# Token sums of the seven-product up projection: formed during two plain f-tiles, the fourth kept in DRAM, and the down phase's loads in another order

## The chip, the cores and the metric

The kernel runs on one core of a Trainium2 chip. A core has TensorE (PE) for matmuls, VectorE (DVE), ScalarE (ACT), GpSimd (POOL) and SyncE (SP), which issues nearly all DMAs of this kernel. The metric is the device time of one execution in microseconds (us), lower being better; three runs of the kernel before have a median of 2636.69 us.

## The reference: what is computed

One inference step of a streaming encoder with two layers, in fp32, for 1152 tokens (a prompt of 1024 and 8 running streams of 16) of width 1024. Layer 0 mixes tokens by a gated recurrence beside a differential attention, layer 1 by trailing-window means. Behind either mixer stands the same feed-forward block, and the change is in that block alone. The width of its hidden layer, D_FF, is 2816:

```python
def conv_ffn(x, hist, w_up, conv_w, conv_b, w_down):
    T = x.shape[1]
    a, b = jnp.split(x @ w_up, 2, axis=-1)
    ah = jnp.concatenate([hist.astype(x.dtype), a], axis=1)
    c = conv_b
    for j in range(CONV_W):
        c = c + ah[:, j:j + T] * conv_w[j]
    return (jax.nn.silu(c) * b) @ w_down, ah[:, -(CONV_W - 1):]
```

Its result is added to the scaled input, and the sum is normalised over the width.

## The kernel before

**Products of three.** An fp32 operand is kept as two parts, `hi` (the value cast to fp32r) and `lo` (the rest). `split` makes them: ACT casts `hi`, VectorE subtracts to get `lo` (GpSimd does it for most weights, by `split_half`). `mm3` then issues three matmuls: hi by hi, hi by lo, lo by hi. The activations stand transposed in SBUF as `xh` and `xl`, 8 blocks of 128 rows (k = 0 to 7) by 1152 tokens.

**The up phase (`ffn_up`).** The 22 f-tiles of 128 hidden columns come one after another. The first two (`PLAIN = 2`, L1180) are plain: for the two halves a and b of `w_up`, three chunks of 384 tokens and 8 blocks of k, 144 matmuls of 128x384. The other 20 use seven products in place of eight (`SEVEN`, L1183), the tokens being cut into halves h0 and h1 and k into two halves: 168 matmuls of 128x288 per f-tile, in the order x00, t3, t2, x10, t1, t4, x11 of their token operands. The first three token sums t1, t2 and t3 have tiles of their own and are made by `combine(kk)` (L1273) for each of the four slices kk of 128x576, one slice behind each of the first four chunks of the second plain tile. t4 takes the place of x01, that is `xh` and `xl` at [0:4, h1], which plain tiles still read; so `combine_last(kk)` (L1285) makes it behind the last plain tile, during the first four products.

The weights of each seven-product tile are loaded by `fetch` (L1302) to one of three `raw` tiles and summed and split by `prepare` (L1309), five products ahead (`AHEAD`): VectorE forms the sums (L1320 to L1324), ACT `hi`, GpSimd `lo`. The results of a tile are gathered in `ext` (the half a) and `bb` (the half b), in part by ACT's copies and in part by VectorE's additions (L1375 to L1385). `conv(f)` (L1212) makes the convolution, SiLU and the product with `bb` from them, beside the next f-tile, and stores the row f of 128x1152 in DRAM as `g_scr`.

**The down phase (`ffn_down`).** It reads the rows of `g_scr` back (`graw`, one buffer, 576 KB), splits them into `gh` (ACT) and `gl` (VectorE), and adds their products with `w_down` into nine tiles `acc` of 512 KB, which hold the block's input, loaded from `x_scr`. Rows come in groups of two. Its first loads are emitted inside the up phase: `leave()`, two products before its end, frees the tiles of t1 to t3 and runs `ffn_down` to its first `yield`; `open_acc` opens the nine tiles and loads them, each `fetch` loads a row's weights and its `graw`.

```python
1406         acc = open_acc(lambda t: scr_rows(l, t))
...
1442         ready = [fetch(f) for f in GROUPS[0]]
1443         yield acc
```

**What sets the order.** A scheduler places the instructions on the engines by their dependencies and the order in which they are emitted; each engine then works through its own queue in order, and SP's DMAs start in SP's order. A tile with one buffer is rewritten only when its last reader is done.

Of the kernel before, what the change touches and what calls it, by code (L numbers as in the profile page):

```python
# [10 lines left out]
F32 = mybir.dt.float32  # L11
F32R = mybir.dt.float32r
# [98 lines left out]
def hybrid_stream_kernel(ctx: ExitStack, tc: tile.TileContext, i, o, k):  # L111
# [42 lines left out]
    def split(hi, lo, src, sub=None):  # L154
        nc.scalar.copy(hi, src)  # L155
        (sub or nc.vector).tensor_tensor(lo, src, hi, ALU.subtract)  # L156

    def raw_tile(name="raw"):
        return wp.tile([128, 1024], F32, tag="raw", name=name, bufs=3)
# [108 lines left out]
    def drain(g):  # L268
        for _ in g:
            pass  # L270

    def chain(*gens):
        for g in gens:
            yield from g
# [16 lines left out]
    oa_scr = dr.tile([NTOK, 512], F32, name="oa_scr")  # L291
    ob_scr = dr.tile([NTOK, 512], F32, name="ob_scr")
    x_scr = [dr.tile([NTOK, D], F32, name=f"x_scr{l}") for l in range(2)]
    g_scr = [dr.tile([NF, 128, NTOK], F32, name=f"g_scr{l}") for l in range(2)]
    w_in = i["w_in_ab"][0].rearrange("(k p) c -> p k c", p=128)

# [778 lines left out]

    acc_s = []

    def open_acc(rows):

        acc_s.append(ExitStack())  # L1080
        accp = pool_of(acc_s[0], "accp", 1)
        tiles = [accp.tile([128, D], F32, name=f"acc{t}") for t in range(NT)]
        for t in range(NT):
            nc.sync.dma_start(tiles[t], rows(t))
        return tiles

    def close_acc():
        acc_s.pop().close()
# [1 line left out]
    def scr_rows(l, t):  # L1090
        return x_scr[l][t * 128:(t + 1) * 128, :]

    with ExitStack() as ph:
# [42 lines left out]
        last_gate = gate(NPT, so.tile([128, H, 128], F32, tag="gate", name="gt"))  # L1136
        drain(running)
        at_s.close()
        acc = open_acc(x_rows)
        sp = pool_of(ph, "sp", 2, side="right")  # L1140
        sums = sp.tile([128, NT, 4], F32, name="sums", bufs=1)

# [34 lines left out]


    HALF = NTOK // 2
    PLAIN = 2  # L1180


    SEVEN = (("a0", "x00", 0, True), ("s3", "t3", 1, True), ("s2", "t2", 0, False), ("a1", "x10", 2, True),  # L1183
# [3 lines left out]
    def ffn_up(l, acc, late, first, leave):  # L1187
# [44 lines left out]
        def plain(f, w, order):  # L1232

            _, _, bb = begin(f)
            for part, c in order:
                a, n = CHUNKS[c]
                p = bank([128, n], "pu")
                for kk in range(KD):
                    mm3(p, w[part][0][kk], w[part][1][kk], xh[:, kk, a:a + n], xl[:, kk, a:a + n],
                        kk == 0, kk == KD - 1)  # L1240
                if part == 0:
                    put_a(f, a, p, n)
                else:
                    nc.vector.tensor_copy(bb[:, a:a + n], p)
                yield
# [24 lines left out]
        def temp(n):  # L1270
            return tmp.tile([128, HALF], F32, tag=n, name=n)

        def combine(kk):  # L1273

            A, B, C = temp("sa"), temp("sb"), temp("sc")
            nc.vector.tensor_tensor(A, xh[:, kk, h0], xl[:, kk, h0], ALU.add)
            nc.gpsimd.tensor_tensor(B, xh[:, kk, h1], xl[:, kk, h1], ALU.add)
            nc.gpsimd.tensor_tensor(C, xh[:, 4 + kk, h1], xl[:, 4 + kk, h1], ALU.add)
            nc.vector.tensor_tensor(A, B, A, ALU.subtract)
            nc.vector.tensor_tensor(B, C, B, ALU.subtract)  # L1280
            nc.vector.tensor_tensor(C, C, A, ALU.subtract)
            for n, src in (("t3", B), ("t2", C), ("t1", A)):
                split(tt[n][0][:, kk], tt[n][1][:, kk], src)

        def combine_last(kk):  # L1285
            A, B = temp("sa"), temp("sb")
            nc.gpsimd.tensor_tensor(A, xh[:, 4 + kk, h0], xl[:, 4 + kk, h0], ALU.add)
            nc.vector.tensor_tensor(B, tt["t2"][0][:, kk], tt["t2"][1][:, kk], ALU.add)
            nc.vector.tensor_tensor(A, A, B, ALU.subtract)
            split(xh[:, kk, h1], xl[:, kk, h1], A)  # L1290

        def tokens(n, q, c):
            cs = slice(c * (HALF // 2), (c + 1) * (HALF // 2))
# [8 lines left out]
        def fetch(f, part):  # L1302
            raw = raw_tile()
            nc.sync.dma_start(raw.rearrange("p (k c) -> p k c", c=128), up_cols(l, part * FF + f * 128))
            raws[f, part] = raw
# [20 lines left out]
                   "s3": b[:, up], "s4": a[:, lo]}[name]  # L1326
            wts[n] = [x.rearrange("p (k c) -> p k c", c=128) for x in split_half(src)]

        u = plain(1, second, [(p, c) for p in range(2) for c in range(3)])
        side = conv(0)  # L1330
        for s in range(6):
            next(u)
            if s < 4:
                combine(s)
            if s in (0, 2):
                next(side, None)
            if s in (1, 2):
                fetch(PLAIN, s - 1)
            if s >= 4:
                prepare(s - 4)  # L1340
        drain(u)
        drain(side)
        fetch(PLAIN + 1, 0)
        for n in range(2, AHEAD):
            prepare(n)

        banks = {}
        n_last = 7 * (NF - PLAIN) - 1
        side = conv(1)
        H2 = HALF // 2  # L1350
        for n in range(n_last + 1):
            f, m = PLAIN + n // 7, n % 7
            if m == 0:
                begin(f)
            if n < 4:
                combine_last(n)
            prepare(n + AHEAD)
            if m == 0 and f + 1 < NF:
                fetch(f + 1, 1)
            if m == 2 and f + 2 < NF:  # L1360
                fetch(f + 2, 0)
            _, tok, bi, starts = SEVEN[m]
            ext, _, bb = open_f[f]
            wh, wl = wts.pop(n)
            for c in range(2):
                if starts:
                    banks[bi, c] = bank([128, H2], "pu")
                p = banks[bi, c]
                for q in range(4):
                    th, tl = tokens(tok, q, c)  # L1370
                    mm3(p, wh[:, q], wl[:, q], th, tl, starts and q == 0, q == 3)
                a0, a1 = c * H2, HALF + c * H2
                e0, b0, b1 = ext[:, 2 + a0:2 + a0 + H2], bb[:, a0:a0 + H2], bb[:, a1:a1 + H2]
                if m == 0:
                    nc.scalar.copy(e0, p)  # L1375
                elif m == 1:
                    nc.scalar.copy(b1, p)
                elif m == 2:
                    nc.scalar.copy(b0, p)
                elif m == 3:  # L1380
                    nc.vector.tensor_tensor(e0, e0, p, ALU.add)
                elif m == 4:
                    nc.vector.tensor_tensor(b1, b1, p, ALU.add)  # L1383
                elif m == 5:
                    nc.vector.tensor_tensor(b0, b0, p, ALU.add)  # L1385
                else:
                    put_a(f, a1, p, H2)
            if n == n_last - 2:
                tmp_s.close()
                tt_s.close()  # L1390
                leave()
            if m in (0, 1, 2, 3, 4):
                next(side, None)
            if m == 6:
                drain(side)
                side = conv(f)
# [5 lines left out]
    def ffn_down(l, last, ahead):  # L1402


        d_s = ExitStack()
        acc = open_acc(lambda t: scr_rows(l, t))
        cp = pool_of(d_s, f"fc{l}", 2)
        gpools = [pool_of(d_s, f"ga{l}", 2)]

# [30 lines left out]
                yield  # L1440

        ready = [fetch(f) for f in GROUPS[0]]
        yield acc
        gpools.append(pool_of(d_s, f"gb{l}", 2, side="right"))
        cq = pool_of(d_s, f"fd{l}", 1, side="right")
# [220 lines left out]
```

## Time and profile before

| | before |
|---|---|
| median of three runs | 2636.69 us (2636.11 to 2640.91) |
| the profiled execution | 2637.27 us |
| its span | 2635.1 us |
| granted TensorE clock, mean | 0.976 |
| TensorE busy | 2514.0 us, 95% of the span |
| VectorE busy | 1561.9 us, 59% |
| ScalarE, GpSimd busy | 1080.1 us, 960.6 us |

The up phase of layer 0 is read here around 925 to 1050 us of the span, where plain tiles give way to seven-product ones, and around 1414 to 1443 us, where the down phase follows. The same places of layer 1 lie at 1858 us and 2337 us. In a table by stretch, busy time is given for each engine with its count of instructions; the granted clock is a share of full speed, so 1.00 is 2.4 GHz. A matmul's row in a timeline shows when it started and how long it lasted; since matmuls overlap, the time from one start to the next is what one costs. Times in square brackets are what the engine was idle just before, and whom it waited for.

### The profile page before, as it was taken

How to read it: one execution, taken by the hardware profiler on the slowest of the kernel's cores; microseconds unless marked ns; L12 is line 12 of the kernel's file. 1: busy time of each engine (PE TensorE's matmuls, PEld its weight loads, DVE VectorE, ACT ScalarE, POOL GpSimd, SP SyncE). 2: the span in 40 equal slices, each digit the busy share in tenths (PEclk: the TensorE clock that was granted, in tenths of full speed). 3: DMA queues.
4: the chain of work that ended last, by engine and by line, in shares of the span. 5: the costliest groups of instructions: out<-in, count | busy, mean ns of one | idle time of the engine just before them, and what ended most of it. 6: DMA issues, size and time to landing. Idle time of an engine off the chain costs nothing. (4 is left out here: it accounts for less than half of the span.)

```text
span 2635.1 us, 45541 instructions
## 1 busy us (share of the span) xinstructions
PE 2514.0 (95%) x18138; PEld 2309.4 (88%) x18138; DVE 1561.9 (59%) x2728; ACT 1080.1 (41%) x2192; POOL 960.6 (36%) x735
## 2 busy tenths in 40 slices
PE   8999999999999889999998999989799999989997
PEld 8999987886889889999997788879799999977886
DVE  3377753338983685555554665788755555456557
ACT  2255545355762534444443121365344444431113
POOL 1111111006642555554553122244555555521222
PEclk9999999998999989999999999989899999999998
DMA  5744357777674212222224222232122222252222
GB/s 167 200 115 121 87 171 248 221 256 241 230 229 174 104 35 66 76 76 76 76 76 182 89 94 83 69 92 81 51 76 76 76 75 76 75 186 96 93 77 81
DMA packets 275123, 314.36 MB, mean 119 GB/s; under 512 B 46059, under 2 KB 209460, under 8 KB 274911
## 3 DMA queue, kind: packets, MB, share of 16 engines
q1 hardware_dynamic: 272485, 309.82, 36.2%
q8 instruction: 143, 2.34, 0.4%
q10 hardware_dynamic: 2426, 1.63, 0.3%
q14 instruction: 69, 0.57, 0.1%
HBM read 239.66 MB, written 71.74 MB: 118 GB/s over the span
## 5 line engine op out<-in xcount | busy, mean ns | idle before, releaser
L156 POOL TENSOR_TENSOR lo<-raw,hi 128x512 fp32r<-128x512 f32 x364 | 517.1, 1433 | 1128.5 <-ACT hi L155 985.3
L155 ACT CAST hi<-raw 128x512 fp32r<-128x512 f32 x380 | 231.6, 620 | 573.3 <-PE pu L143 275.9
L143 PE MATMUL pu<-xh,hi 128*128 128x288 f32 (+1 forms) x1472 | 444.9, 303 | 9.9 <-DVE bb L1383 9.4
L143 PE MATMUL pu<-xl,hi 128*128 128x288 f32 (+1 forms) x1472 | 444.4, 302 | 3.0 <-DVE xl L156 3.0
L143 PE MATMUL pu<-xh,lo 128*128 128x288 f32 (+1 forms) x1472 | 444.2, 302 | 0.0
L143 PE MATMUL pd<-hi,gh 128*128 128x512 f32 x792 | 315.7, 399 | 21.7 <-ACT gh L155 21.7
L143 PE MATMUL pd<-lo,gh 128*128 128x512 f32 x792 | 317.2, 401 | 0.0
L143 PE MATMUL pd<-hi,gl 128*128 128x512 f32 x792 | 313.3, 396 | 0.0
L1435 DVE TENSOR_TENSOR acc<-acc,pd 128x512 f32<-128x512 f32 x330 | 216.6, 682 | 122.5 <-PE pd L143 122.2
L143 PEld LDWEIGHTS pu<-xh,hi 128*128 128x128 f32 x1472 | 278.8, 190 | 11.3 <-DVE bb L1383 10.4
L143 PEld LDWEIGHTS pu<-xl,hi 128*128 128x128 f32 x1472 | 279.2, 190 | 3.6 <-DVE xl L156 3.6
L143 PEld LDWEIGHTS pu<-xh,lo 128*128 128x128 f32 x1472 | 279.2, 190 | 0.0
L143 PE MATMUL ptm<-hi,xh 128*128 128x256 f32 x720 | 209.5, 291 | 4.2 <-ACT hi L155 4.2
L143 PEld LDWEIGHTS pd<-hi,gh 128*128 128x128 f32 x792 | 150.2, 190 | 60.4 <-ACT gh L155 22.6
L143 PE MATMUL ptm<-lo,xh 128*128 128x256 f32 x720 | 202.1, 281 | 0.1
L143 PE MATMUL ptm<-hi,xl 128*128 128x256 f32 x720 | 201.9, 281 | 0.0
L1222 DVE SCALAR_TENSOR_TENSOR cv<-ext,prm,cv 128x1024 f32<-128x1024 f32 (+1 forms) x176 | 178.0, 1066 | 28.9 <-ACT cv L1219 28.8
L143 PEld LDWEIGHTS pd<-hi,gl 128*128 128x128 f32 x792 | 149.8, 189 | 36.7 <-DVE gl L156 1.2
L143 PEld LDWEIGHTS pd<-lo,gh 128*128 128x128 f32 x792 | 150.1, 190 | 34.3
L143 PEld LDWEIGHTS ptm<-hi,xh 128*128 128x128 f32 x720 | 136.5, 190 | 7.4 <-ACT hi L155 4.6
L143 PEld LDWEIGHTS ptm<-lo,xh 128*128 128x128 f32 x720 | 136.6, 190 | 0.9 <-DVE lo L156 0.4
L143 PEld LDWEIGHTS ptm<-hi,xl 128*128 128x128 f32 x720 | 136.2, 189 | 0.0
(332 smaller groups left out, 5886.3 us busy)
## 6 DMA issues: line engine op xcount, KB each, us to landing
raw<-in_ffn_w_up SPq DMA_DIRECT2D x88, 512.0 KB
kraw<-in_cache_k SPq DMA_DIRECT2D x64, 512.0 KB
vraw<-in_cache_v SPq DMA_DIRECT2D x64, 512.0 KB
g_scr<-cv SPq DMA_DIRECT2D x44, 576.0 KB
graw<-g_scr SPq DMA_DIRECT2D x44, 576.0 KB
raw<-in_ffn_w_down SPq DMA_DIRECT2D x44, 512.0 KB
raw<-in_w_in_ab SPq DMA_DIRECT2D x28, 512.0 KB
x_scr<-acc SPq DMA_DIRECT2D x18, 512.0 KB
```

Of the source, the lines that this page charges most:

```text
L143: nc.tensor.matmul(out, a, b, start=start, stop=stop, skip_group_check=True)
L155: nc.scalar.copy(hi, src)
L156: (sub or nc.vector).tensor_tensor(lo, src, hi, ALU.subtract)
L1222: nc.vector.scalar_tensor_tensor(dst, tap[j], cw[j], dst, ALU.mult, ALU.add)
L1435: nc.vector.tensor_tensor(acc[t][:, cs], acc[t][:, cs], p, ALU.add)
```

## The change

- Three f-tiles per layer are plain (`PLAIN = 3`), 19 use seven products. The third tile's weights (`third`) are loaded by `load_up` behind the fifth chunk of the second tile.
- `combine` has become a generator with four steps and also makes t4: from GpSimd's sum of x10 (L1291 of the new kernel) and `sc`, which still holds the slice's t2. Its two parts go to two `raw` tiles and from there to a new DRAM buffer `t4_scr`, two stores of 128x576 per slice. The steps of the four slices run two behind each chunk of the second tile and one behind each chunk of the third.
- `swap()` behind the third plain tile loads `xl` and then `xh` at [0:4, h1] from `t4_scr`, two DMAs of 128x4x576. `combine_last` is gone.
- In `ffn_down` the tiles `acc` are opened where they were, and loaded (`load_acc`) behind the fetches of the first group.

```diff
@@ ffn_up
-    PLAIN = 2
+    PLAIN = 3
@@ combine
         nc.vector.tensor_tensor(C, C, A, ALU.subtract)
-            for n, src in (("t3", B), ("t2", C), ("t1", A)):
+            yield
+            for n, src in (("t3", B), ("t1", A), ("t2", C)):
                 split(tt[n][0][:, kk], tt[n][1][:, kk], src)
-
-        def combine_last(kk):
+            yield
             A, B = temp("sa"), temp("sb")
             nc.gpsimd.tensor_tensor(A, xh[:, 4 + kk, h0], xl[:, 4 + kk, h0], ALU.add)
-            nc.vector.tensor_tensor(B, tt["t2"][0][:, kk], tt["t2"][1][:, kk], ALU.add)
-            nc.vector.tensor_tensor(A, A, B, ALU.subtract)
-            split(xh[:, kk, h1], xl[:, kk, h1], A)
+            nc.vector.tensor_tensor(B, A, C, ALU.subtract)
+            parts = [raw_tile("t4") for _ in range(2)]
+            split(*[r[:, 0:HALF].bitcast(F32R) for r in parts], B)
+            yield
+            for n in range(2):
+                nc.sync.dma_start(t4_scr[l][kk, n], parts[n][:, 0:HALF])
+
+        def swap():
+            for n, x in enumerate((xh, xl)):
+                nc.sync.dma_start(x[:, 0:4, h1].bitcast(F32), t4_scr[l][:, n].rearrange("k p t -> p k t"))
@@ behind the first plain tile
-        u = plain(1, second, [(p, c) for p in range(2) for c in range(3)])
-        side = conv(0)
-        for s in range(6):
-            next(u)
-            if s < 4:
-                combine(s)
-            if s in (0, 2):
-                next(side, None)
-            if s in (1, 2):
-                fetch(PLAIN, s - 1)
-            if s >= 4:
-                prepare(s - 4)
-        drain(u)
+        both = [(p, c) for p in range(2) for c in range(3)]
+        side = chain(*[combine(kk) for kk in range(4)])
+        third = []
+        for f, w in ((1, second), (2, third)):
+            u = plain(f, w, both)
+            cv = conv(f - 1)
+            for s in range(6):
+                next(u)
+                if s in (0, 2):
+                    next(cv, None)
+                if f == 1 and s == 4:
+                    third += [load_up(l, 256), load_up(l, FF + 256)]
+                if f == 2 and s in (1, 2):
+                    fetch(PLAIN, s - 1)
+                if f == 2 and s >= 4:
+                    prepare(s - 4)
+                for _ in range(2 if f == 1 else 1):
+                    next(side, None)
+            drain(u)
+            drain(cv)
         drain(side)
+        swap()
         fetch(PLAIN + 1, 0)
...
-            if n < 4:
-                combine_last(n)
             prepare(n + AHEAD)
@@ ffn_down
-        acc = open_acc(lambda t: scr_rows(l, t))
+        acc = open_acc()
...
         ready = [fetch(f) for f in GROUPS[0]]
+        load_acc(acc, lambda t: scr_rows(l, t))
         yield acc
```

How this moves the instructions on the engines, in the order in which each engine has them:

SP at the change from plain to seven-product tiles in layer 0, first before (`g_scr` is a finished row, `in_ffn_w_up` weights):

```order
L1304 DMA raw<-in_ffn_w_up 128x8x128
L240 DMA x_scr_94<-acc_10204 128x1024
L1304 DMA raw<-in_ffn_w_up 128x8x128
L1230 DMA g_scr_96<-cv 128x1152
L1304 DMA raw<-in_ffn_w_up 128x8x128 x2
L1230 DMA g_scr_96<-cv 128x1152
```

and after (`t_scr_96` is the DRAM buffer of t4, L171 the load of the third tile's weights):

```order
L171 DMA raw<-in_ffn_w_up 128x8x128 x2
L1297 DMA t_scr_96<-t_11700 128x576
L1297 DMA t_scr_96<-t_11701 128x576
L1297 DMA t_scr_96<-t_11751 128x576
L1297 DMA t_scr_96<-t_11752 128x576
L1315 DMA raw<-in_ffn_w_up 128x8x128 x2
L1233 DMA g_scr_98<-cv 128x1152
L1315 DMA raw<-in_ffn_w_up 128x8x128 x2
L1301 DMA xl<-t_scr_96 128x4x576
L1301 DMA xh<-t_scr_96 128x4x576
L1315 DMA raw<-in_ffn_w_up 128x8x128
```

Two slices' stores of t4 and the first four weight loads now stand ahead of the two loads of the swap; the first two slices' stores (not printed here) stand ahead of the load of the third tile's weights.

VectorE at the first slice in layer 0, before (`sa`, `sb` and `sc` are the temporaries, L156 the `lo` of a split):

```order
L1279 TENSOR_TENSOR sa<-sb,sa 128x576
L1280 TENSOR_TENSOR sb<-sc,sb 128x576
L156 TENSOR_TENSOR t1l<-sa,t1h 128x576
L1281 TENSOR_TENSOR sc<-sc,sa 128x576
L156 TENSOR_TENSOR t3l<-sb,t3h 128x576
L1276 TENSOR_TENSOR sa<-xh,xl 128x576
L156 TENSOR_TENSOR t2l<-sc,t2h 128x576
```

and after:

```order
L1283 TENSOR_TENSOR sa<-sb,sa 128x576
L1284 TENSOR_TENSOR sb<-sc,sb 128x576
L156 TENSOR_TENSOR t1l<-sa,t1h 128x576
L1285 TENSOR_TENSOR sc<-sc,sa 128x576
L156 TENSOR_TENSOR t3l<-sb,t3h 128x576
L1292 TENSOR_TENSOR sb<-sa,sc 128x576
L156 TENSOR_TENSOR t2l<-sc,t2h 128x576
L1280 TENSOR_TENSOR sa<-xh,xl 128x576
L1225 SCALAR_TENSOR_TENSOR cv<-ext,prm_68,cv 128x1024
```

The subtraction for t4 (L1292) stands inside the slice, and the convolution of the first f-tile follows the first slice.

SP where the down phase of layer 0 begins, before (L171 is the last of the first weight loads, `acc_...` the nine tiles):

```order
L171 DMA raw<-in_ffn_w_down 128x1024
L1084 DMA acc_16536<-x_scr_94 128x1024
L1084 DMA acc_16537<-x_scr_94 128x1024
L1084 DMA acc_16538<-x_scr_94 128x1024
L1084 DMA acc_16539<-x_scr_94 128x1024
L1084 DMA acc_16540<-x_scr_94 128x1024
L1084 DMA acc_16541<-x_scr_94 128x1024
L1084 DMA acc_16542<-x_scr_94 128x1024
L1084 DMA acc_16543<-x_scr_94 128x1024
L1084 DMA acc_16544<-x_scr_94 128x1024
L1413 DMA graw<-g_scr_96 128x1152
```

and after:

```order
L171 DMA raw<-in_ffn_w_down 128x1024
L1430 DMA graw<-g_scr_98 128x1152
L1087 DMA acc_16502<-x_scr_94 128x1024
L1087 DMA acc_16503<-x_scr_94 128x1024
L1087 DMA acc_16504<-x_scr_94 128x1024
L1430 DMA graw<-g_scr_98 128x1152
L1087 DMA acc_16505<-x_scr_94 128x1024
```

The first row of g stands ahead of all nine `acc` loads, the second behind three of them; five more `acc` loads follow the last row printed.

## Rows read from the trace of the kernel before

**Rows 1.** The page: busy time, share of the span and instructions of each engine

```profile
PE 2514.0 (95%) x18138; PEld 2309.4 (88%) x18138; DVE 1561.9 (59%) x2728; ACT 1080.1 (41%) x2192; POOL 960.6 (36%) x735
```

**Rows 2.** TensorE's waits, 955:1027: waiter, released by; us in total, times, longest

```profile
PE pu L143 <- ACT ext L1375: 5.0, 1, 5.0
PE pu L143 <- DVE bb L1383: 4.7, 2, 4.0
PE pu L143 <- ACT hi L155: 4.3, 1, 4.3
```

**Rows 3.** Stretches: us, busy PE PEld DVE ACT POOL, clock, DMA share, GB/s

```profile
955.80:1027.35 71.55, 56.10 (x361) 54.59 (x361) 45.59 (x61) 26.74 (x53) 37.65 (x29) 0.86 0.20 61
1858.19:1928.74 70.55, 54.04 (x361) 52.53 (x361) 44.41 (x61) 26.74 (x53) 37.33 (x28) 0.88 0.20 62
1027.35:1049.62 22.27, 22.27 (x170) 22.27 (x169) 11.96 (x18) 9.57 (x19) 11.63 (x10) 1.00 0.23 74
```

**Rows 4.** TensorE's timeline, seven-product tiles: start us, us, instruction

```profile
955.80 0.29 PE L143 MATMUL pu<-xh,hi 128*128 128x288 f32 x1
...
1027.35 0.30 PE L143 MATMUL pu<-t3h,hi 128*128 128x288 f32 x1
```

**Rows 5.** TensorE's timeline, second plain tile, two matmuls 96 apart

```profile
937.26 0.34 PE L143 MATMUL pu<-xl,hi 128*128 128x384 f32 x1
...
953.90 0.34 PE L143 MATMUL pu<-xl,hi 128*128 128x384 f32 x1
```

**Rows 6.** VectorE's timeline, slices of token sums and the first weight sum

```profile
924.61 1.97 DVE L1279 TENSOR_TENSOR sa<-sb,sa 128x576 f32<-128x576 f32 x1 [0.95 <-POOL sb L1277]
...
928.02 1.85 DVE L1281 TENSOR_TENSOR sc<-sc,sa 128x576 f32<-128x576 f32 x1
...
933.73 3.91 DVE L1222 SCALAR_TENSOR_TENSOR cv<-ext,prm,cv 128x1024 f32<-128x1024 f32 x3
...
938.29 0.74 DVE L1280 TENSOR_TENSOR sb<-sc,sb 128x576 f32<-128x576 f32 x1
...
938.96 0.74 DVE L156 TENSOR_TENSOR t1l<-sa,t1h 128x576 fp32r<-128x576 f32 x1
...
959.64 0.68 DVE L1320 TENSOR_TENSOR sa<-raw 128x512 f32<-128x512 f32 x1
```

**Rows 7.** GpSimd's timeline, a sum of one slice

```profile
924.53 1.43 POOL L1278 TENSOR_TENSOR sc<-xh,xl 128x576 f32<-128x576 f32 x1
```

**Rows 8.** SP's queue, the weight loads behind the first weight sums

```profile
970.22 3.48 SPq L1304 DMA_DIRECT2D raw<-in_ffn_w_up  x2
```

**Rows 9.** SP's queue, first loads of the down phase, layer 0

```profile
1418.91 4.77 SPq L1084 DMA_DIRECT2D acc<-x_scr  x9
1424.02 0.32 SPq L1413 DMA_DIRECT2D graw<-g_scr  x1
```

**Rows 10.** ACT's timeline at the start of the down phase, layer 0

```profile
1422.01 0.62 ACT L155 CAST hi<-raw 128x512 fp32r<-128x512 f32 x1 [2.56 <-PE pu L143]
...
1434.46 1.15 ACT L155 CAST gh<-graw 128x1152 fp32r<-128x1152 f32 x1 [2.90 <-DMA graw<-g_scr]
```

**Rows 11.** TensorE's timeline, down phase begins: layer 0, and layer 1's first

```profile
1424.95 0.29 PE L143 MATMUL pu<-xh,lo 128*128 128x288 f32 x1
1435.67 0.79 PE L143 MATMUL pd<-hi,gh 128*128 128x512 f32 x1 [10.42 <-ACT gh L155]
...
1440.49 0.40 PE L143 MATMUL pd<-hi,gl 128*128 128x512 f32 x1
...
1442.83 0.40 PE L143 MATMUL pd<-hi,gh 128*128 128x512 f32 x1
...
2337.46 0.79 PE L143 MATMUL pd<-hi,gh 128*128 128x512 f32 x1 [10.82 <-ACT gh L155]
```

**Rows 12.** The stretch from the first graw load on (columns as rows 3)

```profile
1424.00:1430.00 6.00, 1.25 (x10) 1.01 (x8) 2.64 (x3) 2.60 (x6) 1.53 (x3) 1.00 1.03 419
```

More of the change, by code (lines that the diff above doesn't have):

```diff
@@ L293, in hybrid_stream_kernel @@
     x_scr = [dr.tile([NTOK, D], F32, name=f"x_scr{l}") for l in range(2)]
+    t4_scr = [dr.tile([4, 2, 128, NTOK // 2], F32, name=f"t4_scr{l}") for l in range(2)]
     g_scr = [dr.tile([NF, 128, NTOK], F32, name=f"g_scr{l}") for l in range(2)]
@@ L1076, in hybrid_stream_kernel, with open_acc, load_acc @@
     acc_s = []
-    def open_acc(rows):
+    def open_acc():
         acc_s.append(ExitStack())
         accp = pool_of(acc_s[0], "accp", 1)
-        tiles = [accp.tile([128, D], F32, name=f"acc{t}") for t in range(NT)]
+        return [accp.tile([128, D], F32, name=f"acc{t}") for t in range(NT)]
+    def load_acc(tiles, rows):
         for t in range(NT):
             nc.sync.dma_start(tiles[t], rows(t))
-        return tiles
     def close_acc():
@@ L1138, in hybrid_stream_kernel @@
         at_s.close()
-        acc = open_acc(x_rows)
+        acc = open_acc()
+        load_acc(acc, x_rows)
         sp = pool_of(ph, "sp", 2, side="right")
@@ L1348, in ffn_up @@
         n_last = 7 * (NF - PLAIN) - 1
-        side = conv(1)
+        side = conv(PLAIN - 1)
         H2 = HALF // 2
@@ L1405, in ffn_down @@
         d_s = ExitStack()
-        acc = open_acc(lambda t: scr_rows(l, t))
+        acc = open_acc()
         cp = pool_of(d_s, f"fc{l}", 2)
```

## The prediction

> **What bounds the kernel now.** TensorE is busy 95% of the span [rows 1], so little can come from other engines unless TensorE waits for them. The view of its waits over the stretch in which the up phase of layer 0 changes from plain to seven-product f-tiles shows waits of 4 to 5 us for ACT's copies, VectorE's additions and a weight part [rows 2]. Waits understate the loss, because the clock falls with them; the table by stretch has both. From the first matmul of the first seven-product tile to the first on t3 in the third tile [rows 4] are 71.55 us with 361 matmul records and a granted clock of 0.86; layer 1 has 70.55 us at 0.88. The next tile of the same work takes 22.27 us at 1.00 [rows 3]. The stretch holds two such tiles and one product more, 22.27 x (2 + 1/7) = 47.7 us. So 23.8 us are lost in layer 0 and 22.8 us in layer 1, **46.7 us** together. The other place is where the down phase begins: TensorE waits 10.42 us in layer 0 and 10.82 us in layer 1 for ACT's gh, the first split of a row of g_scr [rows 11].
>
> **The up phase.** The cause of the stall is VectorE: from 924.6 us on it works through the token sums of four slices, and the sums of the first weights come after them, at 959.64 us [rows 6], when the first seven-product tile is due (955.80 us, [rows 4]); the load that waits for their buffers is issued at 970.22 us [rows 8]. A third plain tile gives this chain more time.
>
> What the tile itself costs: 96 plain matmuls lie between 937.26 and 953.90 us [rows 5], 0.1733 us each; 144 of them are 24.96 us, against 22.27 us for the tile that it replaces. That is +2.69 us per layer, **5.4 us** in all.
>
> When is the new chain done? A slice has nine VectorE operations before the weights' sums where it had seven (the three of combine_last go), 36 in four slices. Undisturbed they take 0.74 us, at a pitch of 0.67 us [rows 6]; with the sums on POOL that are not hidden, 1.43 us each [rows 7], four slices are some 30 us. An operation that runs beside POOL takes 1.85 to 1.97 us [rows 6]; two of those per slice add 4 x 2 x 1.1 = 9 us. VectorE also has the conv of two f-tiles (3.91 us for most of one, [rows 6]; some 11 us with the multiplications and copies, my estimate), and some 3 us for POOL's third weights. From 924.6 us this gives 968.6 to 978 us, middle 973. The plain tiles run until then and further: with the third tile inserted, seven products start at 955.80 + 24.96 + wait = 980.8 us or a little later. So sums t1 to t3 are ready, and the loss in the first two products goes. TensorE's own results of the plain tiles wait for VectorE's bb copies in the same queue, but eight banks of PSUM hold more than a tile of them; I cost that at nothing, and if the cover goes, it is a wait of some 4 us as in [rows 2].
>
> Two new waits come with it. The first is the third tile's weights. Their load stands on SP behind the stores of a t4 slice, so it cannot leave before the second slice is split, about 949 us; a load takes 3 to 4 us, and the split on ACT (0.62 us, [rows 10]) and POOL (1.43 us) follows twice. Ready at 956 to 958 us, needed at 955.80 us: a wait of 0 to 4 us, I take **2 us per layer**.
>
> The second is the swap. It is issued behind the stores of the last slice and, on SP, behind the second weight load of the second seven-product tile, which waits until POOL has split the first tile's sixth weights. In the trace of before a load of that place left 10.6 us after the sums (959.64 to 970.22, [rows 6, 8]). Chain end 973 plus some 5.5 us for the last stores and loads plus 10.6 us is 989 us. It moves 2.36 MB, behind 0.5 MB of weights; at 419 GB/s, the most this trace shows in a stretch like it [rows 12], that is 6.9 us, and with about 1.5 us of start 8.4 us, so t4 is in place at 996 to 998 us, at 1003 us if the chain ends late. TensorE reads t4 in the sixth product: 980.8 + 2 + 5 x 22.27 / 7 = 998.7 us. So 0 to about 4 us are waited, and a wait of over 4 us brings some 2 us of low clock with it, as the down phase shows below. I take **1.5 us per layer**. The stores of t4, 2.36 MB in eight pieces per layer, run while DMA moves 61 GB/s [rows 3] and no engine reads them but the swap: nothing.
>
> Up phase: 46.7 - 5.4 - 4 - 3 = **34.3 us**.
>
> **The down phase.** Before, the first graw load is issued at 1424.02 us, behind nine acc loads that SP issues from 1418.91 us on [rows 9]; those 4.7 MB and the first graw share the queue, at 419 GB/s in 1424 to 1430 us [rows 12], and ACT gets graw only for the split at 1434.46 us [rows 10]. TensorE stops at about 1425.1 us [rows 11]. After, graw is first. It waits only for the t3 tiles, whose last reader is the second product of the last f-tile, five products (5 x 22.27 / 7 = 15.9 us) before TensorE's end. So it can leave before 1418.91 us and lands some 4 us later; its split comes in ACT's queue behind the weight cast at 1422.01 us [rows 10], at 1422.6 to 1423.8 us. TensorE then has work without a break. The 10.42 and 10.82 us go, 21.2 in all. The slow matmuls behind the wait go too: from 1435.67 to 1440.49 us eleven matmuls take 4.82 us, the next ten (1440.49 to 1442.83 us, [rows 11]) 0.234 us each, so 2.25 us; nearly 2 us in layer 1, by the same count. A further 0.5 us wait per layer brings it to **about 26 us**. Next late is the second graw: it stands on SP behind three acc loads, may go when VectorE has made the first gl (about 1425.1 us), and lands at 1427.8 to 1428.7 us if the queue is served in its order; the first row of g keeps TensorE busy for 22 matmuls, to about 1430.3 us. Its split ends at 1429 to 1429.9 us, so the slack is only about a us. If the six acc loads behind it take an equal share, it is some 4 us late with 2 us of low clock in each layer.
>
> **The sum.** The profiled execution took 2637.27 us, within 0.6 us of the median of the three runs, so I set the sum against it: 2637.27 - 34.3 - 26 = **2577 us**. With none of the new waits it is 2637.27 - 41.3 - 26 = 2570 us.
>
> **Rivals.** (1) *The chain ends late and the swap with it.* For it: operations of 1.85 us beside POOL are common in this stretch, and POOL is busy for 37.65 of 71.55 us [rows 3]. Against it: that POOL work includes the t4 and weight sums, and the chain has 25 us more. A swap at 1003 to 1004 us costs 4.5 to 5 us and 2 us of clock, 7 us per layer in place of 1.5: 2577 + 11 + 2 for the later weights = **2590 us**.
>
> (2) *The down phase gives only half.* The second graw shares DMA with the acc loads and TensorE waits some 4 us with 2 us of low clock per layer: 2577 + 13 = **2590 us**; if the first wait stays too, 2603 us. For it: DMA is full there, share 1.03 [rows 12]. Against: all these loads stand in one queue, and the graw that stood last of ten in it was split last, 10.4 us after its issue.
>
> (3) *Slower: each VectorE operation of the chain meets POOL.* Then 36 operations take 1.85 us [rows 6] in place of 0.75, +39.6 us; the chain ends at 924.6 + 30 + 14 + 39.6 = 1008 us, the swap lands at 1032 us, and TensorE waits 33 us for it and what comes ahead of it, with 3 us of low clock. Per layer that is 36 us in place of 3.5: 2577 + 65 = **2642 us**. It decides against the change from a wait of 32 us per layer on. Against it: POOL is busy for half of the stretch, and of the slice's rows here four are at 0.74 and 0.68 us and only two at 1.85 and more. The Trainium skill, page "SBUF — State Buffer", section "Who interferes with whom", says that a VectorE instruction with two SBUF inputs contends with a GpSimd instruction that reads SBUF and that the loser is blocked for the whole instruction; all operations of the slices are of that kind. By that rule alone the chain would be this long if POOL always had one in flight. The trace agrees on the size (1.85 and 1.97 us against 0.74 us) and not on the frequency.
>
> That the change does not do what it says (the scheduler leaves VectorE's sums where they were) is out: the order of the queues shows the third tile ahead of them.
>
> **Chances.** Main case 0.75, (1) 0.12, (2) 0.09, (3) with all else that ends slower 0.04. The range goes from just below the sum without new waits, 2566 us, to 2600 us, which holds (1) and most of (2). A difference under 0.2% (5.3 us) cannot be told from none here. Faster 0.94, same 0.02, slower 0.04.
>
> **What would show it.** Up: after's stretch from the first seven-product matmul on has a granted clock near 1.00, and the first two tiles take 22 to 25 us each; the wait for xh or xl at the sixth product is under 4 us; the swap is issued at about 989 us. A stall at the third plain tile of over 4 us would make the weights' term wrong. Down: the first pd matmul follows the last pu one with no wait over 1 us, and the acc loads come behind graw. The forecast falls if t4 lands after 1005 us, or if a wait of 4 us or more remains at the start of the down phase.

## The result

| | before | changed |
|---|---|---|
| median of the runs | 2638.32 us (4 runs, 2636.11 to 2640.91) | 2604.98 us (4 runs, 2601.48 to 2608.87) |
| ratio, with its 95% interval | | 0.9874 (0.9856 to 0.9891) |
| the profiled execution | 2637.27 us, span 2635.1 | 2601.48 us, span 2599.7 |
| granted TensorE clock, mean | 0.976 | 0.984 |

The change gained 33 us, with an interval of some 4.6 us to either side. The forecast was 60 us (2577 us, range 2566 to 2600): the sign was right, the size was not, and the time lies above the range.

The stretches of the changed kernel that answer to [rows 3] (same columns). The first and third are the new plain tile of layer 0 and 1; the second and fourth go from the first seven-product matmul to the first on t3 in the next f-tile:

```profile
956.86:986.79 29.93, 25.81 (x145) 25.00 (x145) 20.36 (x24) 8.14 (x14) 14.33 (x9) 1.00 0.33 107
986.79:1022.48 35.69, 27.35 (x193) 26.80 (x193) 19.27 (x27) 15.47 (x31) 22.19 (x17) 0.90 0.43 147
1838.66:1870.15 31.49, 27.36 (x145) 26.55 (x145) 21.24 (x25) 8.25 (x15) 14.33 (x9) 0.95 0.33 106
1870.15:1906.74 36.59, 28.83 (x193) 28.25 (x193) 19.70 (x25) 15.38 (x31) 22.62 (x17) 0.86 0.41 140
```

A plain tile without a stall is 24.96 us, so the third one lost 5.0 us in layer 0 and 6.5 us in layer 1. One seven-product tile and a product are 22.27 x 8 / 7 = 25.45 us [rows 3], so 10.2 and 11.1 us were lost there. In all 32.9 us, against 46.7 us before, and the third tile's own 5.4 us come on top: the up phase gained 46.7 - 32.9 - 5.4 = 8.4 us where 34.3 were forecast. Of TensorE's waits in layer 0 from 920 to 1080 us all but 0.5 us stand under two names (waiter, released by; us in total, times, longest):

```profile
PE pu L143 <- ACT ext L1392: 8.3, 2, 7.1
PE pu L143 <- POOL lo L156: 3.9, 2, 3.1
```

The down phase went as forecast. SP's queue where it begins in layer 0, then ACT's timeline, then TensorE's:

```profile
1410.01 0.42 SPq L1430 DMA_DIRECT2D graw<-g_scr  x1
...
1414.04 2.02 SPq L1087 DMA_DIRECT2D acc<-x_scr  x3
1420.38 0.32 SPq L1430 DMA_DIRECT2D graw<-g_scr  x1
```

```profile
1417.67 1.15 ACT L155 CAST gh<-graw 128x1152 fp32r<-128x1152 f32 x1
...
1424.22 1.16 ACT L155 CAST gh<-graw 128x1152 fp32r<-128x1152 f32 x1 [1.38 <-DMA graw<-g_scr]
```

```profile
1420.09 0.30 PE L143 MATMUL pu<-xh,lo 128*128 128x288 f32 x1
1420.22 0.39 PE L143 MATMUL pd<-hi,gh 128*128 128x512 f32 x1
```

The first graw leaves 4.0 us before the first acc load, its split is ready before TensorE ends the up phase, and the first matmul of the down phase follows the last of the up phase by 0.13 us, where [rows 11] had 10.42 us. The second graw comes to its split 3.8 us after its issue and is split by 1425.4 us, while the first keeps TensorE busy.

### Where the up phase's gain went

The stall of 7.1 us is one of ACT's queue. This is ACT's timeline in the changed kernel at the first seven-product tile, then VectorE's, then TensorE's:

```profile
997.90 1.16 ACT L1227 ACTIVATE cv<-cv 128x1152 f32<-128x1152 f32 x1 [5.52 <-DVE cv L1225]
998.97 1.12 ACT L155 CAST hi<-raw 128x512 fp32r<-128x512 f32 x2
1000.00 0.39 ACT L1392 COPY ext<-pu 128x288 f32<-128x288 f32 x1
1003.90 0.62 ACT L155 CAST hi<-raw 128x512 fp32r<-128x512 f32 x1 [3.51 <-DVE raw L1333]
1004.42 0.39 ACT L1392 COPY ext<-pu 128x288 f32<-128x288 f32 x1
```

```profile
992.24 0.69 DVE L1335 TENSOR_TENSOR raw<-raw,sb 128x512 f32<-128x512 f32 x1 [4.55 <-POOL lo L156]
992.85 2.55 DVE L1225 SCALAR_TENSOR_TENSOR cv<-ext,prm,cv 128x1024 f32<-128x1024 f32 x2
```

```profile
1000.44 0.61 PE L143 MATMUL pu<-t2h,hi 128*128 128x288 f32 x1 [7.12 <-ACT ext L1392]
...
1004.87 0.40 PE L143 MATMUL pu<-t2h,hi 128*128 128x288 f32 x1 [1.22 <-ACT ext L1392]
```

The product with t2 adds into the banks that hold the first product, so ACT's copies of them to ext (L1392) must be done. The first product ended at 989.98 us. But ahead of the copy in ACT's queue stood the SiLU of the third plain tile (L1227). ACT had done what came before it by 992.4 us, and then the SiLU waited 5.52 us for VectorE's convolution, which had itself stood behind a weight sum (L1335) that waited 4.55 us for GpSimd. Everything behind the SiLU stood still, the 0.39 us copy too. The second copy stood behind one more cast, whose weights were loaded and summed only by 1003.9 us. Nobody was overloaded: ACT was busy for 15.47 of these 35.69 us, VectorE for 19.27.

SP's queue shows the other part. The t4 parts lie in the three raw buffers that weights use too, and their stores wait for VectorE:

```profile
951.44 1.16 SPq L171 DMA_DIRECT2D raw<-in_ffn_w_up  x2
960.01 18.49 SPq L1297 DMA_DIRECT2D t_scr<-t  x4
978.61 1.30 SPq L1315 DMA_DIRECT2D raw<-in_ffn_w_up  x2
...
980.80 16.11 SPq L1315 DMA_DIRECT2D raw<-in_ffn_w_up  x2
996.97 0.57 SPq L1301 DMA_DIRECT2D xl<-t_scr  x1
```

The third tile's weights leave at 951.44 us, behind the second slice's stores, the first seven-product tile's only at 978.61 us, after the last t4 store, and the swap at 996.97 us, behind a weight load that waits for its buffer.

### The profile page after: what moved, and what is told of

Same layout as the page of the kernel before. It is cut to its first block, busy times and chain, and to the rows that moved or that the text cites. A ratio compares the mean times of both kernels' runs of the same rounds, so it can differ in the third digit from the quotient of the medians.

```text
span 2599.7 us, 45443 instructions
## 1 busy us (share of the span) xinstructions
PE 2505.4 (96%) x18090; PEld 2301.7 (89%) x18090; DVE 1531.6 (59%) x2706; ACT 1074.1 (41%) x2176; POOL 967.1 (37%) x729
## 5 line engine op out<-in xcount | busy, mean ns | idle before, releaser
L156 POOL TENSOR_TENSOR lo<-raw,hi 128x512 fp32r<-128x512 f32 x362 | 531.6, 1481 | 1103.2 <-ACT hi L155 976.1
L143 PE MATMUL pu<-xh,lo 128*128 128x288 f32 (+1 forms) x1504 | 457.1, 304 | 7.7 <-POOL lo L156 7.7
L143 PE MATMUL pu<-xl,hi 128*128 128x288 f32 (+1 forms) x1504 | 456.5, 304 | 3.0 <-DVE xl L156 3.0
L143 PE MATMUL pu<-xh,hi 128*128 128x288 f32 (+1 forms) x1504 | 457.1, 304 | 1.0 <-ACT hi L155 0.5
L1225 DVE SCALAR_TENSOR_TENSOR cv<-ext,prm,cv 128x1024 f32<-128x1024 f32 (+1 forms) x176 | 183.8, 1099 | 34.8 <-ACT cv L1222 34.8
```

The lines of the kernel that those rows point to most:

```text
L143: nc.tensor.matmul(out, a, b, start=start, stop=stop, skip_group_check=True)
L1225: nc.vector.scalar_tensor_tensor(dst, tap[j], cw[j], dst, ALU.mult, ALU.add)
```

## The experiments

Each row is the median of its own runs and the ratio to the kernel before, timed beside it.

| run | what differs | us | ratio (95%) |
|---|---|---|---|
| e1_up_only | changed, old down order | 2629.6 | 0.9971 (0.9961 to 0.9981) |
| e2_down_only | before, new down order | 2614.6 | 0.9913 (0.9898 to 0.9928) |
| e3_third_early | third weights ahead of t4 stores | 2603.7 | 0.9869 (0.9854 to 0.9883) |
| e4_silu_after | ACT's order, SiLU only | 2602.4 | 0.9869 (0.9854 to 0.9885) |
| e6_silu_swap | ACT's and SP's order | 2594.8 | 0.9836 (0.9821 to 0.9850) |
| e7_silu_swap_s4 | and VectorE's weight sum | 2587.0 | 0.9803 (0.9787 to 0.9819) |
| e8_all | and e3, and the convolution later | 2582.1 | 0.9784 (0.9770 to 0.9799) |
| e11_park_order | e8, and ACT's weight casts | 2581.0 | 0.9780 (0.9765 to 0.9794) |
| e9_no_park | three plain tiles, t4 in place | 2590.9 | 0.9819 (0.9804 to 0.9834) |
| e10_nopark_order | e9 and ACT's order | 2587.3 | 0.9806 (0.9791 to 0.9820) |
| e14_nopark_order_s4 | e10 and VectorE's weight sum | 2584.5 | 0.9794 (0.9781 to 0.9808) |
| e12_two_plain_order | e2 and ACT's order | 2607.0 | 0.9883 (0.9867 to 0.9900) |
| e13_swap_twice | changed, swap issued twice | 2605.7 | 0.9875 (0.9860 to 0.9889) |

Where an order is set by hand, `tc.issue_after(x)` keeps what a block issues on x's engine behind x; it adds no wait.

### The two halves: e1 and e2

```diff
 # e1, on the changed kernel
         acc = open_acc()
+        load_acc(acc, lambda t: scr_rows(l, t))
...
         ready = [fetch(f) for f in GROUPS[0]]
-        load_acc(acc, lambda t: scr_rows(l, t))
```

e2 is the reverse: the kernel before with `load_acc` behind `ready`.

> The changed kernel with the acc loads of the down phase put back ahead of the first graw, so that only the up phase's part is left. My theory: the down phase's order is worth about 25 us and the up phase's part about 10, and they add up. So 2628 us, 10 below the kernel before, with TensorE's two waits of 10 to 11 us for gh back. Rival: the up phase's part alone is worth the forecast 34 us and the new load order costs the rest somewhere else; then 2604 us here.

> The kernel before with the one change that the acc loads stand behind the loads of the first group of the down phase. My theory: 25 to 26 us less, 2613 us, and no wait for gh of over 1 us at the two starts of the down phase; the up phase's waits (ext, bb, hi) as before. Rival: the order gives little by itself, 2625 us or more, because the second graw then waits.

Measured: 2629.6 us, 8.4 below its 2638.0, and 2614.6 us, 23.4 below. In e1 the waits for gh are back; in e2 they are gone and the up phase's waits stand, here for the whole span (two layers), as in [rows 2]. The first row is of e1, the others of e2:

```profile
PE pd L143 <- ACT gh L155: 20.2, 3, 9.9
```

```profile
PE pu L143 <- ACT ext L1377: 9.7, 2, 5.2
PE pu L143 <- DVE bb L1385: 9.4, 4, 4.0
```

So some 70% of the change's gain are the two moved lines of the down phase. The halves add up to 31.8 us, the whole is 33.3.

### The third tile's weights: e3

```diff
-                if f == 1 and s == 4:
+                if f == 1 and s == 0:
                     third += [load_up(l, 256), load_up(l, FF + 256)]
```

> The changed kernel with the weights of the third plain tile loaded behind the first chunk of the second tile and not behind the fifth, ahead of every store of t4. Both theories expect the wait for these weights (3.9 us and 2 us of slow clock per layer) to go. Theory A, the stall behind it is set by a chain that does not depend on it (last t4 store, weights of the first seven-product tile, their sums, then ACT's queue): the 6 us per layer are lost again at the ext copy, which then waits 13 us instead of 7, and the time is within 4 us of the changed kernel's, 2601 to 2606 us. Theory B, the two stalls are independent: 12 us less, 2593 us.

Measured: 2603.7 us, theory A by its time. The weights' wait is gone and the third tile ends early, but other waits take its place. TensorE's waits in layer 0 of e3, 920 to 1080 us:

```profile
PE pu L143 <- ACT ext L1392: 8.4, 2, 7.2
PE pu L143 <- ACT hi L155: 1.9, 1, 1.9
PE pu L143 <- POOL lo L156: 0.8, 1, 0.8
```

The first seven-product tile's weights are loaded at 979.02 us here, as late as in the changed kernel, and the new waits for them take back 2.7 us, the slow clock behind them (thirteen matmuls 0.24 us apart in place of 0.13) some 1.4 us more. So ext did not wait the 13 us that theory A had, but 8.4 us, and the ext copies come when they came (1000.78 us for the first product with t2, 1000.44 us in the changed kernel). Time that is won ahead of a stall with a fixed end was lost again here.

### ACT's queue: e4, and with SP's and VectorE's: e6, e7

```diff
 # e4, at n == 1 of the first seven-product tile; e0_copy is the second of its two ext copies
-                next(side, None)
+                with tc.issue_after(e0_copy.ins):
+                    next(side, None)
 # e6, besides: swapped is the swap's second load
-                fetch(f + 1, 1)
+                with tc.issue_after(swapped):
+                    fetch(f + 1, 1)
 # e7, besides: the weight sum of the second tile (n == 13); added is the first tile's last addition into bb
-                nc.vector.tensor_tensor(a[:, lo], a[:, lo], sums[2], ALU.subtract)
+                with tc.issue_after(added[0]):
+                    nc.vector.tensor_tensor(a[:, lo], a[:, lo], sums[2], ALU.subtract)
```

> The changed kernel with ACT's order alone set by hand: the SiLU of the third plain tile behind the first seven-product tile's two ext copies. SP's order stays, so the cast of the second tile's weights, which cannot come before these are loaded and summed (1003.9 us in layer 0), still stands between the two ext copies. Theory A (what TensorE waits for is the copy's place in ACT's queue, and each instruction ahead of it that waits counts): the first ext copy comes 6 us earlier, the second does not, so the wait moves to the second half of the same product and the time stays within 3 us of the changed kernel's, 2601 to 2606 us. Theory B (the SiLU is the cause, and what stands between the copies costs nothing): 2585 to 2592 us.

> The changed kernel with two places of the queues set by hand: on ACT the SiLU of the third plain tile stands behind the first seven-product tile's two ext copies and not ahead of them; on SP the two loads of the swap stand ahead of the second tile's second weight load, so that the cast of these weights no longer stands between the two ext copies. Theory A (ACT's queue: the ext copies are ready at about 990 us but stand behind a SiLU that waits for VectorE until 997.9 us): the waits of 7.1 and 1.2 us for ext go, with 1.9 us of slow clock, 10 us per layer, and t4 is read without a wait; 2585 us. Theory B (VectorE is so late that whatever TensorE needs next comes late too): the wait moves to bb, to hi or to xl and the time stays above 2598 us.

> The version with the SiLU behind the ext copies and the swap ahead of the second tile's second weight load, and one place more: on VectorE the weight sum of the second tile that waits 4.2 us for GpSimd's lo stands behind the first tile's last addition into bb and not ahead of its second addition into ext. Theory A: the wait of 3.8 us for bb that was left in that version goes with some 2 us of slow clock, 5 to 6 us per layer; 2583 to 2585 us. Theory B (VectorE is loaded too much there, and the additions come late in any order): within 3 us of 2595 us, with the wait at another row of VectorE.

e4 took 2602.4 us, theory A: with the SiLU away the first copy comes 5.4 us earlier (994.55 us, not 1000.00), and the long wait moves to the second copy, behind the cast of weights not yet there. TensorE in e4:

```profile
994.99 0.40 PE L143 MATMUL pu<-t2h,hi 128*128 128x288 f32 x1 [1.22 <-ACT ext L1392]
...
1004.07 0.61 PE L143 MATMUL pu<-t2h,hi 128*128 128x288 f32 x1 [7.23 <-ACT ext L1392]
```

e6 took 2594.8 us: no wait for ext is left, which is theory A's mechanism, but only 10 of the 20 us came, since the wait moved to bb, one of the places that theory B had named. VectorE and TensorE in e6:

```profile
1009.09 1.74 DVE L1336 TENSOR_TENSOR raw<-raw,sb 128x512 f32<-128x512 f32 x1 [4.16 <-POOL lo L156]
...
1011.11 0.81 DVE L1404 TENSOR_TENSOR bb<-bb,pu 128x288 f32<-128x288 f32 x2
```

```profile
1011.61 0.51 PE L143 MATMUL pu<-xh,hi 128*128 128x288 f32 x1 [3.79 <-DVE bb L1404]
```

It is the same pattern on another engine: a weight sum that only the last product of the next tile needs waits for GpSimd, and an addition that TensorE needs at once stands behind it. e7 changes that one place: 2587.0 us, 2 above what was expected, and no wait for bb on VectorE. So theory B's reason, a VectorE too late in any order, does not hold for this wait.

### All places: e8 and e11

e8 takes e7 with e3's early load and puts VectorE's convolution of the second plain tile behind the last slice; e11 also puts the casts of products 6 and 7 behind the ext copies.

> All places together: SiLU and weight sum behind the copies and additions that TensorE waits for, the swap ahead of the second weight load, the third tile's weights loaded ahead of the t4 stores, and VectorE's convolution of the second plain tile behind the last slice of token sums, so that the last t4 store and with it the first seven-product tile's weights come earlier (at about 971 us instead of 978 us in layer 0). Theory A (the up phase's loss was queue order and the shared raw buffers, not VectorE's amount of work): no wait over 1 us from the second plain tile on, and the whole 16 us per layer come back; 2570 to 2577 us, near the forecast. Theory B (amount of work): one of these waits comes back in another place; 2583 us or more.

> The version with all places set and t4 parked, and in addition ACT's casts of the first tile's last and the second tile's first weights behind the two ext copies (the first of them waits for a sum on VectorE, and that for GpSimd). Theory A: its last wait for ext, 2.6 us per layer, goes with some 1 us of slow clock; 2573 to 2577 us, what the sum gives without any stall (2571 us) but for the wait of 0.5 us for lo. Theory B: the wait moves to bb or to a weight; 2580 us or more.

e8 took 2582.1 us, between the theories and close to B's bound of 2583 us: the last store no longer waits until 978 us, though the weights' load leaves at 976.01 us and not at 971 us, the third tile has no wait, and what remains in each layer is

```profile
PE pu L143 <- ACT ext L1405: 2.6, 1, 2.6
PE pu L143 <- POOL lo L156: 0.5, 1, 0.5
```

e11 took 2581.0 us, the fastest here and faster than both kernels, but not to be told from e8. It went as theory B had it: the wait for ext shrank to 0.2 us in that place, and 1.6 us came back at bb (TensorE's waits of e11 in layer 1):

```profile
PE pu L143 <- ACT bb L1413: 1.8, 2, 1.6
```

So 23 to 24 us of the 28 missed came back by the places of instructions in their queues, with no change in what is computed. The last 11 us to the prediction's sum without new waits (2570 us) were not reached; that these small waits and the clock behind them are all of it was not shown.

### Is parking needed: e9, e10, e14

e9 keeps three plain tiles and the new down order, but forms t4 in place by `combine_last` during the first four products; no store, no swap. e10 and e14 set its order as above.

> The changed kernel without parking: three plain tiles and the new order of the down phase, but t4 is formed during the first four seven-product products as before, with no store, no t4 tiles among the raw buffers and no swap. Theory A (the third tile gives VectorE the time; parking moves work ahead but ties up the raw buffers and SP, and the ext copies wait in ACT's queue either way, here behind the casts of t4): about the same time, 2598 to 2610 us, with no wait for the third tile's weights and a longer one for ext. Theory B (forming t4 early is what gained): the old stall of 23 us per layer comes back in good part, 2618 us or more.

> The version without parking (three plain tiles, t4 formed in place during the first products), with ACT's order set by hand: the two ext copies of the first seven-product tile stand ahead of the third tile's SiLU, of the second to fourth cast of t4 and of the weight casts of later products. Theory A (the 6.3 us per layer that version still waits are places in ACT's queue): they go with some 2 us of slow clock per layer; 2573 to 2577 us. Theory B (VectorE has too much work there to form t4 in time): a wait for xl (t4) or bb takes their place; 2585 us or more.

> The version without parking and with ACT's order set, and in addition VectorE's weight sum of the second tile behind the first tile's last addition into bb. It still waited 4.9 us for bb in the version before it, because that sum stands ahead of one of the additions and waits 3.8 us for GpSimd. Theory A (order was all that was left, and parking gains nothing once the order is right): 6 to 7 us less per layer, 2573 to 2577 us, 4 to 8 us below the best version with parking. Theory B (forming t4 in place takes VectorE time in the stretch that parking keeps free, and parking is worth that): the wait moves to xl or stays at bb, 2581 us or more.

e9 took 2590.9 us, 14 us less than the changed kernel and 7 less than theory A's lower end; the old stall of theory B did not come back. Without t4 parts in the raw buffers, weights come early: no wait but for ext is left, and the two of 3 us stand behind casts of t4 that wait for VectorE. ACT and TensorE in e9:

```profile
999.41 0.67 ACT L155 CAST xh<-sa 128x576 fp32r<-128x576 f32 x1 [4.41 <-DVE sa L1295]
999.99 0.39 ACT L1388 COPY ext<-pu 128x288 f32<-128x288 f32 x1
```

```profile
995.06 0.40 PE L143 MATMUL pu<-t2h,hi 128*128 128x288 f32 x1 [3.23 <-ACT ext L1388]
...
1000.44 0.61 PE L143 MATMUL pu<-t2h,hi 128*128 128x288 f32 x1 [3.02 <-ACT ext L1388]
```

e10 (2587.3 us) removed these and met the same weight sum on VectorE, as theory B had it, 4.9 us for bb per layer; e14 (2584.5 us) removed that one and kept smaller waits for ext, bb and xl, 4 to 5 us per layer without those that stand ahead of the stretch. Theory A had both at 2573 to 2577 us and missed; both times lie where theory B had them. But theory B's reason in e14, that parking is worth something, is not shown: with the order set, parking (2581 us) and no parking (2584.5 us) cannot be told apart. With the order as the scheduler leaves it, parking costs 14 us.

### Is the third tile needed: e12; what the swap costs: e13

> The kernel before with the down phase's new order and ACT's order set by hand as in the version without parking, but with two plain tiles: what order alone does without a third tile. Theory A (the third tile is needed too, since VectorE's chain of slices ends after the first seven-product tile is due, and the waits for hi and bb come from that): 8 to 14 us off the version with the new down order alone, 2600 to 2607 us, with waits for hi and bb or xl left. Theory B (order is all): 2575 to 2585 us.

> The changed kernel with the two loads of the swap issued twice in a row, 4.7 MB in place of 2.4 MB. Theory A (t4 lands some 7 us before its product, since TensorE is held up before it by ext): 6 us more of transfer stay hidden, no wait for xh or xl of over 1 us, within 3 us of the changed kernel's 2605 us. Theory B (the swap stands on the path): 5 to 7 us per layer more, 2615 us or more, with a wait for the DMA of xl or xh at the sixth product.

e12 took 2607.0 us, theory A: order alone takes 7.6 us off e2 (8 to 14 were expected), and the wait of 4.3 us for hi stays, since with two plain tiles VectorE's chain is late. The waits for VectorE's bb are gone. But at its first product with t2 TensorE still waits for ext, 4.0 us in layer 0 and 3.5 us in layer 1: the first cast of t4, which this order leaves ahead of the copies, waits for VectorE. ACT in e12:

```profile
973.23 0.67 ACT L155 CAST xh<-sa 128x576 fp32r<-128x576 f32 x1 [7.46 <-DVE sa L1291]
```

e13 took 2605.7 us: the second pair stayed hidden but for 0.5 and 0.8 us in the two layers. SP in e13, and TensorE's first matmul on t4:

```profile
998.98 0.57 SPq L1301 DMA_DIRECT2D xl<-t_scr  x1
...
1005.31 0.36 SPq L1301 DMA_DIRECT2D xl<-t_scr  x1
1008.37 0.36 SPq L1301 DMA_DIRECT2D xh<-t_scr  x1
```

```profile
1015.58 0.40 PE L143 MATMUL pu<-xh,hi 128*128 128x288 f32 x1 [0.47 <-DMA xh<-t_scr]
```

The second load of xl can start only when the first has landed, so one swap takes 6.3 us for xl and 8.8 us for xh. In the changed kernel, issued at 996.97 us, it lands at about 1006 us, and TensorE reads t4 at 1012.93 us.

## Why the prediction was wrong, step by step

**Right: the down phase.** Forecast 26 us, alone 23.4 us (e2, whose interval of 19 to 27 us holds 26), with both long waits gone and the second graw in time as worked out. So the second rival, a second graw that shares DMA and comes late, did not occur: TensorE waited 0.2 us there.

**Right: the price of a third plain tile, and the sums.** Third-tile matmuls come every 0.174 us; t1 to t3 were in place in time. VectorE's chain ended at 978.2 us, at the late end of 968.6 to 978 us.

**Wrong: "the loss in the first two products goes".** This is the step that failed. It took the stall of [rows 2] for one cause, VectorE's chain, and let it go whole once the sums were early. But the first row there names ACT's ext copy, 5.0 us, and a copy also waits for its place: it stands in ACT's queue behind instructions that wait for others, in the changed kernel a SiLU and a cast of weights. The third tile did not change that; with the chain over at 978 us, the copy still came at 1000 us. The wait became 8.3 us, and with the slow clock 10.2 and 11.1 us per layer were lost where nothing was put down; e6 and e7 removed it by order alone, for 18 us. The stores of t4, also put at nothing, had a part in it: they kept the weights, and with them the SiLU, late. In e9, which has no stores, 14 us come back in the scheduler's own order; since either cure works on the same loss, the 14 and the 18 us do not add up. It could have been found before: for each releaser in the waits, look at what stands ahead of it in its own queue, and whom that waits for. In the kernel before, too, ACT's ext copies came right behind a cast of t4 that waited for VectorE. That its place alone made the wait of 5.0 us there was not shown, since e12 left this cast ahead of the copies. ACT's timeline of before:

```profile
973.93 0.67 ACT L155 CAST xh<-sa 128x576 fp32r<-128x576 f32 x1 [3.65 <-DVE sa L1289]
974.51 0.69 ACT L1375 COPY ext<-pu 128x288 f32<-128x288 f32 x2
```

**Mis-sized: the third tile's weights.** 2 us per layer in the sum, 5.0 and 6.5 measured. The load left at 951.44 us, close to what was worked out (about 949 us), but GpSimd's queue had been left out: three of its four los for them stand behind a slice's sum that waits for VectorE. GpSimd's timeline of the changed kernel:

```profile
960.02 1.86 POOL L1282 TENSOR_TENSOR sc<-xh,xl 128x576 f32<-128x576 f32 x1 [1.37 <-DVE t2l L156]
961.84 5.26 POOL L156 TENSOR_TENSOR lo<-raw,hi 128x512 fp32r<-128x512 f32 x3
```

Nor was the term worth what it measured: e3 removed it and gained nothing that can be told (1.3 us), because the end of the next stall did not move with it.

**Mis-sized the other way: the swap.** 1.5 us per layer in the sum, none measured. Its issue was later than worked out (997 us, not 989), and t4 landed at about 1006 us, past the 1005 us that the prediction gave as a sign of its failing; but TensorE was held up longer. The 8.4 us for the transfer were about right (8.8 us for both loads in e13), though no row shows the 1.5 us of start in them. That the rivals' numbers (2590 us, and 2603 us for the second at its worst) lie nearer to 2605 us than the forecast is therefore chance: of the first the late chain end was right, but its stall at t4 did not occur, and of the second nothing occurred. The raw buffers were seen as a resource of the swap's weight load only; that the t4 parts shut the weights out of two of three was missed.

**The rule on the shared port.** Of 35 slice operations on VectorE in 922 to 979 us of the changed kernel 4 took over 1.4 us (such as 1.95 us at 949.04 us, the others about 0.75 us), each of them beside a GpSimd instruction of 1.3 to 1.9 us. So the Trainium skill, page "SBUF — State Buffer", section "Who interferes with whom", is borne out in what one blocking costs; that every operation of a chain meets one, as the third rival had it, is not. The chain lost more by waiting for GpSimd, 10.4 us in eight waits, most of them for its sums and some 1.3 us long, than by these four, some 4.6 us.

## What to carry to other kernels

When a wait is to be removed, follow it to the releasing instruction and then up that engine's queue: a copy of 0.4 us that must free a PSUM bank is worth what the slowest waiter ahead of it costs. A stall that is removed ahead of another with a fixed end may gain nothing (e3), so find what fixes the last one's end first. And before work is taken off a path by way of memory, see which buffers and which queue it borrows: here t4's parts took the weights' buffers, and in the scheduler's order doing without them was 14 us faster.

## What the runs showed of the hardware

The same wait did not cost the same clock twice. In the third tile TensorE waited 3.06 us for lo in both layers, until 964.14 us and until 1845.94 us; in layer 0 the granted clock stayed at 1.00 (2.4 GHz) behind it, in layer 1 it fell for a time to the lower level (0.83 is the mean of 10 us; columns as in [rows 3]):

```profile
964.14:970.00 5.86, 5.86 (x34) 5.86 (x35) 4.54 (x3) 0.00 (x0) 5.33 (x3) 1.00 0.13 50
...
1846.00:1856.00 10.00, 10.00 (x49) 10.00 (x50) 8.68 (x9) 2.02 (x3) 6.57 (x4) 0.83 0.08 29
```

And where it fell, it could do so after TensorE had run at full speed again: in e8, behind a wait of 2.63 us, five matmuls from 992.62 us on came 0.13 us apart (2.4 GHz) before the next thirteen, from 993.34 us on, came 0.24 us apart (1.2 GHz):

```profile
992.38 0.40 PE L143 MATMUL pu<-t2h,hi 128*128 128x288 f32 x1 [2.63 <-ACT ext L1405]
992.62 0.30 PE L143 MATMUL pu<-t2l,hi 128*128 128x288 f32 x1
...
993.34 0.44 PE L143 MATMUL pu<-t2h,hi 128*128 128x288 f32 x1
993.58 0.44 PE L143 MATMUL pu<-t2l,hi 128*128 128x288 f32 x1
```

The prediction reckoned with the slow clock behind waits of over 4 us only; 2.6 us can be enough, and 3.1 us need not be.
